# Last down-projection part of a decoder block: activations split in place, modulation rows one at a time, late x and partial-sum tiles fetched late

## Chip, cores and metric

One core of one Trainium2 chip runs the whole block. The metric is the device time of one execution in microseconds (us). The kernel before took 2182.07 us in the median of three runs.

## The reference

A decoder block in float32 with 512 tokens and 2048 channels. The part that matters here is its end:

```python
c_act = jax.nn.silu(c)
mod = c_act @ w_ada[l] + b_ada[l]
sh1, sc1, gt1, sh2, sc2, gt2 = jnp.split(mod[:, None, :], N_MOD, axis=-1)
...
h = _rmsnorm(x, norm2_g[l]) * (1.0 + sc2) + sh2
x = x + gt2 * _conv_ffn(h, w_up[l], conv_w[l], conv_b[l], w_down[l])
return _rmsnorm(x, norm_f_g)
```

`_conv_ffn` multiplies by `w_up`, convolves over three tokens, gates, and multiplies the 5632 gated channels by `w_down`. This last product, the gate vector `gt2` (the last 2048 columns of `w_ada`) and the final normalisation are the kernel's last stage.

## The kernel before

Channels lie on the 128 partitions and tokens on the free axis. Every float32 product is made of three TensorE passes (`mm3`, L133 to L135): a matrix is split into a rounded high part and the remainder, and high by high, high by low and low by high are added up in PSUM. Splitting a weight tile (`wsplit`) takes one ScalarE cast (L1373) and one VectorE subtraction (L1374); three split buffers `uw` take turns, so the split of one tile can run while two earlier ones are in use.

The 44 channel blocks of the down-projection come in three groups. Blocks 0 to 7 are a plain product, whose sums go to DRAM (`yd`). Blocks 8 to 23 are done by a Strassen-Winograd scheme (`strassen`, eight steps of seven half-width products), whose results are added to `yd` in DRAM by accumulating DMAs. Blocks 24 to 43, the last part, are 20 blocks kept as ten pairs `A3`. `act_pair` loads a pair from DRAM (`ad`) into two scratch slots of 128x512, and casts and subtracts into an operand unit that the Strassen scheme has given free; `REST` lists which unit each pair takes: first those of Y11, then Y21, T1, T2 and T3. The first four pairs are made inside the last Strassen step (`in_last`), the others in `down_four`. There are ten slots in all, which serve every short-lived 128x512 tile.

There are 16 output tiles f. For f = 0 to 3, `down_four` goes over blocks 0-7, then 8-15, then 16-19, and for each of these over the four tiles, so that the late pairs are needed late. Tiles 4 to 7 follow one by one, 512 tokens wide. Tiles 8 to 15 are done in two halves of 256 tokens (`down_half`), so that the first half can be normalised while the second is multiplied. A product over 8 blocks and 512 tokens is 24 matmuls of 128x512.

A tile's result is x + gt2 * (yd + last part). `load_x2` fetches the x tile and the `yd` tile by GpSimd's DMA queue and adds gt2*yd on VectorE (L1807); `last_residual` adds the product (L1250), takes squares on ScalarE and adds them up (L1242). The gate column comes from `gate_row`: one row block of `ada3` (128x2048, 1 MB, tile `wa2`) is loaded by SyncE's queue (L1771), multiplied by the broadcast `cact` (tile `cb2`) and summed on VectorE (L1772). Rows i and i+8 are done together in `gate_rows`, row i in buffer `y2` and row i+8 in buffer `y3` (for i under 8), each loaded just ahead of its use in the program. `gate_rows` is called five times in `down_four` and three times in tiles 4 to 6, so 16 rows are done by tile 6.

A scheduler orders each engine's instructions from the program's dependences and its own estimates. After that each engine and each DMA queue works strictly in its own order. SyncE's queue carries the weight tiles (`wd`, L1757), the activation loads (L1488) and the `ada3` rows in one line, so an issue that waits for a buffer holds up everything behind it. The weight tiles of the last part use five buffers in turn: three of tag `wide`, and the two halves of `wd2`, which lies where Y22's second operand unit was. `cb2` takes Y22's first unit, and `y2` and `y3` are T4's units.

Of the kernel before, what the change touches and what calls it, by code (L numbers as in the profile page):

```python
# [26 lines left out]
NWF = 8  # L27
# [40 lines left out]
def block_kernel(ctx, tc, a, out, stop=None, dbg=None):  # L68
    nc = tc.nc
    V, S, G, PE = nc.vector, nc.scalar, nc.gpsimd, nc.tensor  # L70
# [29 lines left out]
    def cols(name, lo, hi):  # L100
        return vec[:, COLS[name] + lo : COLS[name] + hi]
# [11 lines left out]
    mod = cp.tile([P, 96], F32, tag="mod", name="mod")  # L113
# [17 lines left out]
    def mm3(ps, wh, wl, xh, xl, start, stop, more=False):  # L131

        PE.matmul(ps, wh, xh, start=start, stop=False, skip_group_check=more)  # L133
        PE.matmul(ps, wh, xl, start=False, stop=False, skip_group_check=more)  # L134
        return PE.matmul(ps, wl, xh, start=False, stop=stop, skip_group_check=more)  # L135
# [49 lines left out]
    cact = tc.dram_tile([1, D], F32, name="cact")  # L185
# [47 lines left out]
    wa, raws, land, dma = {}, {}, {}, [3.6]  # L233
# [202 lines left out]
    cb = p0.tile([P, D], F32, tag="cb", name="cb")  # L436
# [752 lines left out]
    rb = ctx.enter_context(tc.tile_pool(name="rb", bufs=1, reuse_waits="tile"))  # L1189
# [5 lines left out]
    def bank():  # L1195
        return psm.tile([P, T], F32, tag="b", name="b")
# [14 lines left out]
    def quad(i, name, dt=F32):  # L1211
        return rb.tile([P, 4, T], dt, tag=f"x2_{i}", name=name)
# [18 lines left out]
    ea = ctx.enter_context(tc.tile_pool(name="ea", bufs=1, reuse_waits="tile"))  # L1231
# [36 lines left out]
    for k0 in range(4, KT, 4):  # L1268
# [98 lines left out]
    def wsplit(src, off=0):  # L1367
        n = src.shape[-1]
        i = nsplit[0] % 3
        nsplit[0] += 1  # L1370
        w = (ea, ea, ub)[i].tile([P, WS], F32R, tag=f"w{i}", name="uw")
        hi, lo = w[:, off : off + n], w[:, 2 * QW + off : 2 * QW + off + n]
        S.copy(hi, src)  # L1373
        lo_of[0] = V.tensor_tensor(lo, src, hi.bitcast(F32), op=ALU.subtract)  # L1374
        return hi, lo
# [83 lines left out]
    ad = [tc.dram_tile([P, T], F32, name=f"ad{j}") for j in range(NF)]  # L1459
# [14 lines left out]
    UNITS = [[(ub, f"{t}{g}") for g in range(2)] for t in ("t1", "t2", "y22", "t3")]  # L1474
    UNITS += [[(ea, "t40"), (ea, "t41")]] + [[(rb, f"y{2 * i + g}") for g in range(2)] for i in range(2)]
    FIRST = [(u, g) for u in (5, 6) for g in range(2)]
    REST = [(u, g) for u in (0, 1, 2, 3, 5) for g in range(2)]
    OPS = dict(zip(("Y11", "Y21", "T1", "T2", "Y22", "T3", "T4"), UNITS))
    ND = 8
    NR = NF - 3 * ND  # L1480

    def act_pair(i, u, g):

        pool, tag = UNITS[u][g]
        t = pool.tile([P, 2, 2, T], F32R, tag=tag, name="act2")
        for n in range(2):
            s_ = Slot("al")
            nc.sync.dma_start(s_.t, ad[2 * i + n])  # L1488
            S.copy(t[:, 0, n, :], s_.t)
# [74 lines left out]
    A1, A3 = [], []  # L1564
# [24 lines left out]
    for n, j in enumerate(order):  # L1589
        wa, wb = wq[2 * (n % 2)], wq[2 * (n % 2) + 1]  # L1590
# [137 lines left out]
            pend = (f + NWF, u2, pa, w22)  # L1728
        return pend

    def rest_pair():
        i = len(A3) // 2
        A3.extend(act_pair(3 * ND // 2 + i, *REST[i]))

    def in_last(f, i):
        if f == NWF - 1:
            rest_pair()

    plain(A1, 0)
    pend = strassen(in_last)  # L1740
# [4 lines left out]
    def down_row():  # L1745
        if nrow[0] % 5 > 2:
            w = wd2[:, nrow[0] % 5 - 3, :]
        else:
            w = wide("wd").rearrange("p a b -> p (a b)")
        nrow[0] += 1  # L1750
        return w

    def down(ps, f, acts, blocks=(0, 8, 16)):
        for k0 in blocks:
            n = min(8, NR - k0)
            w = down_row()
            nc.sync.dma_start(w[:, 0 : n * P], a["wdn"][f, :, (3 * ND + k0) * P : (3 * ND + k0 + n) * P])  # L1757
            wh, wl = wsplit(w[:, 0 : n * P], 16 if acts[0].shape[-1] == HT else 0)
            for k in range(n):
                sl = slice(k * P, (k + 1) * P)  # L1760
                x = acts[k0 + k]
                mm3(ps, wh[:, sl], wl[:, sl], x[:, 0, :], x[:, 1, :], start=k0 + k == 0, stop=k0 + k == NR - 1)

    cb = []

    def gate_row(i):
        if not cb:
            cb.append(ea.tile([P, D], F32, tag="t40", name="cb2"))
            nc.sync.dma_start(cb[0], cact[0:1, :].partition_broadcast(P))
        wa = rb.tile([P, D], F32, tag=f"y{2 + i // 8}", name="wa2")  # L1770
        nc.sync.dma_start(wa, a["ada3"][i, :, :])  # L1771
        V.scalar_tensor_tensor(wa, wa, 1.0, cb[0], op0=ALU.mult, op1=ALU.mult, accum_out=mod[:, 80 + i : 81 + i])  # L1772

    def gate_rows(f):
        with tc.issue_after(lo_of[0].ins):
            gate_row(f)
            gate_row(f + NWF)
        m = mod[:, 80:96].rearrange("p (a b) -> p a b", a=2)[:, :, f]
        V.tensor_add(m, m, cols("b_ada", 80, 96).rearrange("p (a b) -> p a b", a=2)[:, :, f])

    def down_four():

        pss = [bank() for _ in range(4)]
        for k0 in (0, 8, 16):
            while len(A3) < min(k0 + 8, NR):
                rest_pair()
# [16 lines left out]
    def load_x2(f):  # L1803
        G.dma_start(x2(f), x2d[f])
        s_ = Slot("yd")
        G.dma_start(s_.t, yd[f])
        V.scalar_tensor_tensor(x2(f), s_.t, gate(f), x2(f), op0=ALU.mult, op1=ALU.add)  # L1807
        s_.done()
# [17 lines left out]
    for f in range(NWF):  # L1826
        if f == 0:
            pss = down_four()
        elif f >= 4:
            if gated[0] < NWF:  # L1830
                gate_rows(gated[0])
                gated[0] += 1
# [6 lines left out]
    for f in range(NWF, KT):  # L1839
        down_half(0, f)  # L1840
    for f in range(NWF, KT):
        n = f - NWF
# [107 lines left out]
```

## Time and profile before

| quantity | value |
|---|---|
| median of three runs | 2182.07 us (2179.99 to 2186.82) |
| profiled execution | 2190.21 us |
| its span, first to last instruction | 2188.4 us |
| busy TensorE, VectorE, ScalarE, GpSimd | 2125.2, 1676.9, 1046.7, 232.5 us |
| HBM read, written | 432.81 MB, 36.18 MB |

The profile is of one execution and lists busy time by engine. PE is TensorE's matmuls, DVE VectorE, ACT ScalarE, POOL GpSimd, SP SyncE, and a q behind an engine means its sequencer or DMA queue. Matmuls overlap each other, so a PE that is busy all the time can still be at half its rate; counting matmuls in a stretch tells more. "a <- b" behind an idle time says that a's wait ended with b. The time outside the span (launch and end) is 1.8 us.

### The profile page before, as it was taken

To read this page: it belongs to the slowest core of one execution; us is meant where nothing else is said; L and a number is where in the kernel's file an instruction comes from. 1 tells how busy PE (TensorE), PEld (TensorE's weight loads), DVE (VectorE), ACT (ScalarE), POOL (GpSimd) and SP (SyncE) were. 2 spreads that over 40 slices of the span, in tenths; PEclk is the share of its full clock that TensorE was granted. 3 is DMA by queue.
4 is the path that set the end of the run, shared out by engine and by line. 5 is a ranking of instruction groups with operands and counts; after the bars stand their busy time and mean duration, and the time that the engine had idled before them with its cause. 6 is when DMAs were issued, how large, how long until landed. Compare 5 with 4: busy or idle time off the path is not lost.

```text
span 2188.4 us, 44045 instructions
## 1 busy us (share of the span) xinstructions
PE 2125.2 (97%) x17864; PEld 1876.5 (86%) x17864; DVE 1676.9 (77%) x2607; ACT 1046.7 (48%) x1510; POOL 232.5 (11%) x368
## 2 busy tenths in 40 slices
PE   8999999999999999999999999999999999996997
PEld 3577777777768888999999999999999899975897
DVE  7988898888853678888888887777778467768454
ACT  4354444444333466655555555555557344432353
POOL 0012111111100101110010000000000000210000
PEclk9999999999999999999999999999999999998998
DMA  9966666666437666988888877777777444698354
GB/s 392 411 215 197 193 194 178 198 184 191 118 111 260 194 200 210 276 242 247 259 245 250 227 208 204 208 207 211 208 194 229 170 143 124 197 348 314 120 180 168
DMA packets 169998, 471.90 MB, mean 216 GB/s; under 512 B 21361, under 2 KB 29505, under 8 KB 159681
## 3 DMA queue, kind: packets, MB, share of 16 engines
q1 hardware_dynamic: 121522, 354.22, 47.7%
q0 software_dynamic: 27056, 77.10, 17.0%
q10 hardware_dynamic: 21216, 37.76, 5.6%
q8 instruction: 140, 2.29, 0.4%
q14 instruction: 64, 0.52, 0.1%
HBM read 432.81 MB, written 36.18 MB: 214 GB/s over the span
## 4 chain that ended last, share of the span: by engine, by line
PE 74%; issue 10%; DMA 8%; DVE 5%; ACT 2%; POOL 1%; SPq 0%; POOLq 0%; DVEq 0%; ACTq 0%
PE b L135 15%; PE b L133 15%; PE b L134 15%; PE mm L631 10%; PE pf L412 4%; DMA wa<-ada 2%; PE b L1203 2%; PE b L1204 1%; DMA wrow<-wup 1%; DMA wraw<-win 1%; PE pb L1033 1%; DVE war L750 1%; DMA x<-dx 1%; DMA wraw<-wout 1%; DMA wd<-wdn 1%
## 5 line engine op out<-in xcount | busy, mean ns | idle before, releaser
L135 PE MATMUL b<-t,uw 128*128 128x256 f32 x1408 | 388.6, 276 | 0.0
L133 PE MATMUL b<-t,uw 128*128 128x256 f32 x1408 | 388.6, 276 | 0.0
L134 PE MATMUL b<-t,uw 128*128 128x256 f32 x1408 | 388.6, 276 | 0.0
L133 PE MATMUL b<-y,uw 128*128 128x256 f32 x1056 | 293.7, 278 | 2.7 <-ACT uw L1373 2.7
L135 PE MATMUL b<-y,uw 128*128 128x256 f32 x1056 | 293.1, 278 | 0.8 <-DVE uw L1374 0.7
L134 PE MATMUL b<-y,uw 128*128 128x256 f32 x1056 | 292.9, 277 | 0.0
L631 PE MATMUL mm<-ahl,whi 128*128 128x512 f32 x864 | 290.5, 410 | 2.0 <-DVE rk L534 1.4
L134 PEld LDWEIGHTS b<-t,uw 128*128 128x128 f32 x1408 | 264.4, 188 | 0.0
L133 PEld LDWEIGHTS b<-t,uw 128*128 128x128 f32 x1408 | 264.3, 188 | 0.0
L135 PEld LDWEIGHTS b<-t,uw 128*128 128x128 f32 x1408 | 264.3, 188 | 0.0
L1374 DVE TENSOR_TENSOR uw<-r,uw 128x1024 fp32r<-128x1024 f32 x164 | 200.3, 1222 | 77.6 <-ACT uw L1373 77.6
L1374 DVE TENSOR_TENSOR uw<-wquart,uw 128x1024 fp32r<-128x1024 f32 x156 | 190.6, 1222 | 68.1 <-ACT uw L1373 67.7
L135 PE MATMUL b<-act,uw 128*128 128x256 f32 (+1 forms) x608 | 203.8, 335 | 13.5 <-DVE uw L1374 13.5
L1374 DVE TENSOR_TENSOR uw<-wd,uw 128x1024 fp32r<-128x1024 f32 (+1 forms) x112 | 123.9, 1107 | 116.9 <-ACT uw L1373 116.9
L133 PE MATMUL b<-act,uw 128*128 128x256 f32 (+1 forms) x608 | 203.9, 335 | 6.2 <-ACT uw L1373 6.2
L1373 ACT CAST uw<-wquart 128x1024 fp32r<-128x1024 f32 x156 | 164.0, 1051 | 89.0 <-PE b L135 66.1
L134 PE MATMUL b<-act,uw 128*128 128x256 f32 (+1 forms) x608 | 203.2, 334 | 0.0
L133 PEld LDWEIGHTS b<-y,uw 128*128 128x128 f32 x1056 | 199.9, 189 | 3.3 <-ACT uw L1373 3.3
L1373 ACT CAST uw<-r 128x1024 fp32r<-128x1024 f32 x164 | 172.4, 1051 | 61.7 <-PE b L135 61.7
L135 PEld LDWEIGHTS b<-y,uw 128*128 128x128 f32 x1056 | 199.7, 189 | 1.2 <-DVE uw L1374 1.2
L134 PEld LDWEIGHTS b<-y,uw 128*128 128x128 f32 x1056 | 199.7, 189 | 0.1
L631 PEld LDWEIGHTS mm<-ahl,whi 128*128 128x128 f32 x864 | 158.6, 189 | 43.3 <-issue 12.2
(353 smaller groups left out, 4599.4 us busy)
## 6 DMA issues: line engine op xcount, KB each, us to landing
wquart<-wup SPq DMA_DIRECT2D x176, 512.0 KB, 5.3
wa<-ada SPq DMA_DIRECT2D x48, 1024.0 KB, 9.4
war<-ada SPq DMA_DIRECT2D x192, 256.0 KB, 3.7
wd<-wdn SPq DMA_DIRECT2D x64, 512.0 KB, 4.4
wraw<-win ACTq DMA_DIRECT2D x118, 256.0 KB, 4.3
wraw<-wout SPq DMA_DIRECT2D x96, 256.0 KB, 3.5
wquart<-wup POOLq DMA_DIRECT2D x44, 512.0 KB, 7.1
r<-wup SPq DMA_DIRECT2D x44, 512.0 KB, 4.6
```

The costliest lines, as they stand in the source:

```text
L133: PE.matmul(ps, wh, xh, start=start, stop=False, skip_group_check=more)
L134: PE.matmul(ps, wh, xl, start=False, stop=False, skip_group_check=more)
L135: return PE.matmul(ps, wl, xh, start=False, stop=stop, skip_group_check=more)
L412: PE.matmul(pf[n % 2 * 4 + ii], w[:, sl], full[k], start=k == 0, stop=k == KT - 1)
L631: PE.matmul(ps, w[:, sl], x, start=first, stop=k == KT - 1 and i == 2)
L750: V.scalar_tensor_tensor(wa, wa, 1.0, cqs[kq], op0=ALU.mult, op1=ALU.mult, accum_out=modq[:, kq, j : j + 1])
L1033: PE.matmul(pt[HS[e], h, c * 2 * L : (c + 1) * 2 * L], nt[HS[e], s, :], rw[HS[e], s, :, :], start=True, stop=True)
L1203: PE.matmul(ps[:, :].rearrange("p (a b) -> p a b", a=2), wh, x, start=start, stop=False)
L1204: PE.matmul(ps[:, 0:HT], wl, x[:, 0, :], start=False, stop=stop)
L1373: S.copy(hi, src)
L1374: lo_of[0] = V.tensor_tensor(lo, src, hi.bitcast(F32), op=ALU.subtract)
```

## The change

It has four parts, all in the last stage.

- The ten activation pairs are loaded into their final place. `act_pair_inplace` sends the raw block into the half of the operand tile that will hold the remainder, casts from there into the other half, and subtracts in place. No slot is used; instead the load itself now has to wait until TensorE has read the old operand. Pairs 0 to 3 are loaded by GpSimd's queue, the other six by SyncE's.
- The gate rows come one at a time, in the order 0 to 15, alternating between `y2` and `y3`. `gate_load` issues a row's load two rows ahead of its use: rows 0 and 1 after the first tile's first product, row i+2 behind row i. Five rows (instead of ten) are done in `down_four`, two with each of the tiles 4 to 7, and the rest in tiles 8 to 12 of the first half. The bias add is now one column per row (16 of 128x1 instead of 8 of 128x2).
- The broadcast `cact` load and rows 0 and 1 have a fixed place in the program.
- `load_x2(f + 8)` moves out of tiles 0 to 7 to the head of `down_half(0, f)`.

```diff
+    def act_pair_inplace(i, u, g, eng):
+        pool, tag = UNITS[u][g]
+        t = pool.tile([P, 2, 2, T], F32R, tag=tag, name="act2")
+        for n in range(2):
+            raw = t[:, 1, n, :].bitcast(F32)
+            eng.dma_start(raw, ad[2 * i + n])
+            S.copy(t[:, 0, n, :], raw)
+            V.tensor_tensor(t[:, 1, n, :], raw, t[:, 0, n, :].bitcast(F32), op=ALU.subtract)
+        return [t[:, :, n, :] for n in range(2)]
...
-    def gate_row(i):
-        if not cb:
-            cb.append(ea.tile([P, D], F32, tag="t40", name="cb2"))
-            nc.sync.dma_start(cb[0], cact[0:1, :].partition_broadcast(P))
-        wa = rb.tile([P, D], F32, tag=f"y{2 + i // 8}", name="wa2")
-        nc.sync.dma_start(wa, a["ada3"][i, :, :])
-        V.scalar_tensor_tensor(wa, wa, 1.0, cb[0], op0=ALU.mult, op1=ALU.mult, accum_out=mod[:, 80 + i : 81 + i])
...
+    def gate_load(i):
+        if i < KT:
+            wa2[i] = rb.tile([P, D], F32, tag=f"y{2 + i % 2}", name="wa2")
+            nc.sync.dma_start(wa2[i], a["ada3"][i, :, :])
+
+    def gate_row():
+        i = gated[0]
+        gated[0] += 1
         with tc.issue_after(lo_of[0].ins):
-            gate_row(f)
-            gate_row(f + NWF)
...
+            m = mod[:, 80 + i : 81 + i]
+            V.scalar_tensor_tensor(wa2[i], wa2[i], 1.0, cb[0], op0=ALU.mult, op1=ALU.mult, accum_out=m)
+            V.tensor_add(m, m, cols("b_ada", 80 + i, 81 + i))
+        gate_load(i + 2)
...
-                if (k0 == 0 and f >= 2) or (k0 == 8 and f % 2 == 0) or (k0 == 16 and f == 0):
-                    gate_rows(gated[0])
-                    gated[0] += 1
+                    cb.append(ea.tile([P, D], F32, tag="t40", name="cb2"))
+                    nc.sync.dma_start(cb[0], cact[0:1, :].partition_broadcast(P))
+                    gate_load(0)
+                    gate_load(1)
+                if k0 // 2 + f > 1 and f % 2:
+                    gate_row()
...
-        load_x2(f + NWF)
         ps = pss[f] if f < 4 else bank()
         if f >= 4:
             down(ps, f, A3)
+            gate_row()
         last_residual(f, [ps], 0, T)
     for f in range(NWF, KT):
+        if gated[0] < KT and f % 2 == 0:
+            gate_row()
+        load_x2(f)
         down_half(0, f)
```

TensorE's order stays as it was. On SyncE's queue, the rows below begin just behind the first four `ada3` rows of before, and end with the first weight tile of tile 4 (the one 128x1024 `wd`). The 128x512 `wd` rows are blocks 16-19 of tiles 0 to 3, and `al` is the last of the activation loads. Before:

```order
L1771 DMA wa_21803<-ada 128x2048
L1771 DMA wa_21806<-ada 128x2048
L1488 DMA al<-ad_9820 128x512
L1757 DMA wd_21569<-wdn 128x512
L1771 DMA wa_21868<-ada 128x2048
L1771 DMA wa_21871<-ada 128x2048
L1757 DMA wd_21569<-wdn 128x512
L1757 DMA wd<-wdn 128x512
L1771 DMA wa_21938<-ada 128x2048
L1771 DMA wa_21941<-ada 128x2048
L1757 DMA wd<-wdn 128x512
L1757 DMA wd<-wdn 128x1024
```

Now, behind the first three rows, up to the seventh; `act` is the last pair's loads:

```order
L1500 DMA act_21883<-ad_9819 128x512
L1782 DMA wa_21812<-ada 128x2048
L1500 DMA act_21883<-ad_9820 128x512
L1768 DMA wd_21561<-wdn 128x512 x2
L1768 DMA wd<-wdn 128x512 x2
L1768 DMA wd<-wdn 128x1024
L1782 DMA wa_21874<-ada 128x2048
L1768 DMA wd_21561<-wdn 128x1024
L1768 DMA wd_21561<-wdn 128x512
L1782 DMA wa_21924<-ada 128x2048
```

Tile 4's first weight tile stood behind ten `ada3` rows and stands behind four now.

On VectorE, the rows below lead up to the remainder of that same weight tile (the last `uw<-wd` row 128x1024). Before:

```order
L1374 TENSOR_TENSOR uw<-wd,uw 128x512
L1779 TENSOR_TENSOR mod<-mod,vec 128x2
L1250 SCALAR_TENSOR_TENSOR x_21570<-b,mod,x_21570 128x512 x2
L1807 SCALAR_TENSOR_TENSOR x_21571<-yd,mod,x_21571 128x512
L1807 SCALAR_TENSOR_TENSOR x_21573<-yd,mod,x_21573 128x512
L1242 TENSOR_TENSOR acc<-acc,sqx 128x512
L1250 SCALAR_TENSOR_TENSOR x_21570<-b,mod,x_21570 128x512
L1772 SCALAR_TENSOR_TENSOR wa_22045,mod<-wa_22045,cb_21695 128x2048
```

and then, behind one more L1250, one more row product L1772 (`wa_22048`), two L1242 and a bias add, `L1374 TENSOR_TENSOR uw<-wd,uw 128x1024`. Now:

```order
L1374 TENSOR_TENSOR uw<-wd,uw 128x512
L1789 SCALAR_TENSOR_TENSOR wa_21874,mod<-wa_21874,cb_21629 128x2048
L1250 SCALAR_TENSOR_TENSOR x_21562<-b,mod,x_21562 128x512
L1790 TENSOR_TENSOR mod<-mod,vec 128x1
L1789 SCALAR_TENSOR_TENSOR wa_21924,mod<-wa_21924,cb_21629 128x2048
L1242 TENSOR_TENSOR acc<-acc,sqx 128x512
L1250 SCALAR_TENSOR_TENSOR x_21562<-b,mod,x_21562 128x512
L1790 TENSOR_TENSOR mod<-mod,vec 128x1
L1822 SCALAR_TENSOR_TENSOR x_21563<-yd,mod,x_21563 128x512
L1250 SCALAR_TENSOR_TENSOR x_21562<-b,mod,x_21562 128x512
L1242 TENSOR_TENSOR acc<-acc,sqx 128x512
L1374 TENSOR_TENSOR uw<-wd,uw 128x1024
```

Two row products still stand between the last 128x512 remainder and this one, now rows 4 and 5 instead of rows 5 and 13 (the eleventh and twelfth that are done); the L1250 of tiles 1 to 3 stand there in both.

More of the change, by code (lines that the diff above doesn't have):

```diff
@@ L1729, in strassen, with rest_pair @@
         return pend
-    def rest_pair():
+    def rest_pair(eng):
         i = len(A3) // 2
-        A3.extend(act_pair(3 * ND // 2 + i, *REST[i]))
+        A3.extend(act_pair_inplace(3 * ND // 2 + i, *REST[i], eng))
     def in_last(f, i):
         if f == NWF - 1:
-            rest_pair()
+            rest_pair(G)
     plain(A1, 0)
@@ L1764, in block_kernel @@
     cb = []
-    def gate_row(i):
-        if not cb:
-            cb.append(ea.tile([P, D], F32, tag="t40", name="cb2"))
-            nc.sync.dma_start(cb[0], cact[0:1, :].partition_broadcast(P))
-        wa = rb.tile([P, D], F32, tag=f"y{2 + i // 8}", name="wa2")
-        nc.sync.dma_start(wa, a["ada3"][i, :, :])
-        V.scalar_tensor_tensor(wa, wa, 1.0, cb[0], op0=ALU.mult, op1=ALU.mult, accum_out=mod[:, 80 + i : 81 + i])
-    def gate_rows(f):
+    wa2 = {}
+    def gate_load(i):
[5 more added lines that the diff above has]
+        gated[0] += 1
         with tc.issue_after(lo_of[0].ins):
-            gate_row(f)
-            gate_row(f + NWF)
-        m = mod[:, 80:96].rearrange("p (a b) -> p a b", a=2)[:, :, f]
-        V.tensor_add(m, m, cols("b_ada", 80, 96).rearrange("p (a b) -> p a b", a=2)[:, :, f])
+            m = mod[:, 80 + i : 81 + i]
+            V.scalar_tensor_tensor(wa2[i], wa2[i], 1.0, cb[0], op0=ALU.mult, op1=ALU.mult, accum_out=m)
+            V.tensor_add(m, m, cols("b_ada", 80 + i, 81 + i))
+        gate_load(i + 2)
     def down_four():
@@ L1785, in down_four @@
             while len(A3) < min(k0 + 8, NR):
-                rest_pair()
+                rest_pair(nc.sync)
             for f in range(4):
```

6 lines of the change are left out of this document (2 added, 4 removed).

## Prediction

> **What bounds the kernel now.** I read the windows of the last 290 us first, then the waits, then the chain of waits. Each window row gives its length, then the busy time and count of PE, PEld, DVE, ACT and POOL, the granted TensorE clock, the DMA share and GB/s.
>
> ```profile
> 1922.24:1960.64 38.40, 36.71 (x172) 29.90 (x171) 22.33 (x26) 9.52 (x13) 6.75 (x11) 1.00 0.96 350
> 1960.64:1978.70 18.06, 13.46 (x58) 10.81 (x58) 15.41 (x18) 2.40 (x5) 2.18 (x4) 0.95 0.95 346
> 1978.70:2007.40 28.70, 16.29 (x49) 12.09 (x50) 24.07 (x31) 8.87 (x13) 2.74 (x5) 0.68 0.90 336
> 2007.40:2059.17 51.77, 51.77 (x229) 42.86 (x228) 26.14 (x31) 14.67 (x17) 0.00 (x0) 1.00 0.44 143
> 2059.17:2171.60 112.43, 112.43 (x967) 112.28 (x965) 63.73 (x85) 59.64 (x80) 0.00 (x0) 1.00 0.56 183
> 1922.24 0.40 PE L133 MATMUL b<-act,uw 128*128 128x512 f32 x1
> 2059.17 0.28 PE L133 MATMUL b<-act,uw 128*128 128x256 f32 x1
> L135 PE MATMUL b<-act,uw 128*128 128x512 f32 x160 | 64.5, 403 | 12.5 <-DVE uw L1374 12.5
> 1902.40:1922.24 19.84, 17.08 (x146) 16.87 (x145) 14.76 (x21) 13.91 (x22) 4.18 (x7) 1.00 0.96 309
> ```
>
> The 512-token part runs from 1922.24 to 2059.17, so 136.9 us. Its fourth window is full: 229 matmuls in 51.77 us, 0.226 us each. In the part, three passes of 160 matmuls take 480 x 0.226 = 108.5 us. The Strassen scheme's last product, 24 matmuls of 128x256, also lies in it: the last row gives (19.84 - 2.76) / 146 = 0.117 us each, where 2.76 us is a wait quoted below, so 2.8 us. Pure work is 111.3 us; 25.6 us are lost. They fall in the second and third windows, where 58 and 49 matmuls stand in 46.8 us, while the DMA engines are over 90% busy at about 340 GB/s. Before and after, TensorE sets the pace.
>
> Who is waited for (total, times, longest):
>
> ```profile
> PE b L135 <- DVE uw L1374: 12.5, 4, 11.2
> PE b L133 <- ACT uw L1373: 6.2, 3, 4.6
> PE b L133 <- ACT cap L1705: 2.8, 1, 2.8
> SPq L1771 <- DVE wa L1772: 50.9, 13, 6.9
> ...
> 1968.68 7.34 DMA wa<-ada
> ...
> 1976.05 1.95 DVE wa L1772
> ...
> 1978.38 7.33 DMA wa<-ada
> ...
> 1985.73 1.29 DVE wa L1772
> ...
> 1988.95 11.33 DMA wd<-wdn
> 1999.36 1.05 ACT L1373 CAST uw<-wd 128x1024 fp32r<-128x1024 f32 x1 [5.24 <-DMA wd<-wdn]
> 2001.65 2.95 DVE L1374 TENSOR_TENSOR uw<-wd,uw 128x1024 fp32r<-128x1024 f32 x3
> ```
>
> PE waits for split weights, these for weight loads, and these for SyncE's queue, which spends 50.9 us waiting until DVE has used up an `ada3` row and freed its buffer. The chain shows this ring: load 7.3, product 2.3, the next load, a round of 1978.38 - 1968.68 = 9.7 us for two rows. Weight loads get through only between rounds; tile 4's (issued 1988.95) lands 11.3 us later.
>
> **The change part by part.** Prices, from the groups and the DMA issues (KB, median us to landing):
>
> ```profile
> L1772 DVE SCALAR_TENSOR_TENSOR wa<-wa,cb 128x2048 f32<-128x2048 f32 x16 | 36.6, 2288 | 11.1 <-DMA wa<-ada 11.0
> L1374 DVE TENSOR_TENSOR uw<-wd,uw 128x1024 fp32r<-128x1024 f32 x18 | 21.9, 1221 | 23.5 <-ACT uw L1373 23.5
> L1807 DVE SCALAR_TENSOR_TENSOR x<-yd,mod,x 128x512 f32<-128x512 f32 x16 | 11.6, 746 | 0.1
> L1250 DVE SCALAR_TENSOR_TENSOR x<-b,mod,x 128x512 f32<-128x512 f32 x8 | 5.9, 746 | 1.6 <-PE b L135 1.6
> L1242 DVE TENSOR_TENSOR acc<-acc,sqx 128x512 f32<-128x512 f32 x6 | 4.1, 687 | 2.9 <-ACT sqx L1241 2.7
> wa<-ada SPq DMA_DIRECT2D x15, 1024.0 KB, 7.4
> wd<-wdn SPq DMA_DIRECT2D x8, 512.0 KB, 9.7
> yd<-yd POOLq DMA_DIRECT2D x14, 256.0 KB, 6.8
> ```
>
> *Rows spread out.* Tile 4's first weight load now stands behind four rows instead of ten: three rounds, 29 us, leave its way, more than the whole loss, so something else comes last. Walking the new order: the last Strassen product ends 8 us after the part's start, near 1930, and frees both buffers. Row 0 lands near 1938 and is used by 1941; only then does SyncE issue row 2 and, behind it, the weights of tiles 2 and 3 for blocks 8-15. With 9.7 us they land at 1951 and are split by 1954. Without waits PE reaches tile 2 there at 1922.2 + 2.8 + 6 x 5.43 = 1957.6. That fits with 3 us to spare. The last activation pair waits for row 1 (used near 1948) and lands at 1956; its remainder precedes tile 3's on DVE, done by 1959 against a need at 1963. Blocks 16-19 end at 1979.5.
>
> There one wait stays. DVE's order has row products 4 and 5, then the last L1250, which needs tile 3's product, and an L1242 ahead of tile 4's remainder. From 1979.5: L1250 0.75, L1242 0.69, L1374 1.22, so 2.7 us; under 0.5 of it is hidden by the two passes that need no remainder. I take 2.7. Tiles 4 to 7 need 13.6 us each (60 x 0.226) and use two rows each, a ring of 9.7, with remainders ordered well ahead: nothing more. Expected loss in the part: 2.7 instead of 25.6, a gain of 22.9.
>
> The clock: the third window was granted 0.68 because of an 11.2 us wait, while the 2.76 us wait near 1916 left the clock at 1.00. A stall of 2.7 should leave it too. The Trainium skill's page "TensorE: Matmul & The Clock Gate", What's actually happening, puts the drop to half rate behind one idle window of about 3.4 us. By that rule, too, 2.7 us costs no clock; a stall a little longer would add some 2.3 us.
>
> *x and `yd` of late tiles.* Eight `yd` loads (2 MB) and, by 1979.5, four rows fewer (4 MB) leave the saturated stretch: about 6 MB, 18 us at 340 GB/s. The `x` loads stay early in GpSimd's queue. What must land from 1918 to 1979.5 is about 18 MB (six rows 6.3, weights 4.7, eleven `act` loads 2.9, `cb2` 1, four `x` tiles 1, five `yd` loads 1.3, two stores 0.5, by the KB of the rows; blocks 0-7 of tiles 0 and 1 are there already): 53 us of 61. That is the thin cover; each load that lands late by more than 3 us costs its excess. I allow 2 us, between 0 and 8 (if the mean rate were 275 GB/s, 18 MB would take 65 us, 4 us too many, and the clock another 4).
>
> *Half stage.* It takes two row products and eight L1807 more, 10.6 us of DVE, beside 63.73 busy of 112.43.
>
> ```profile
> 2070.35 1.23 DVE L1374 TENSOR_TENSOR uw<-wd,uw 128x1024 fp32r<-128x1024 f32 x1 [1.68 <-ACT uw L1373]
> 2073.18 1.23 DVE L1374 TENSOR_TENSOR uw<-wd,uw 128x1024 fp32r<-128x1024 f32 x1 [1.60 <-ACT uw L1373]
> ```
>
> A tile of 7 us leaves DVE two holes, 1.68 and 1.60. A row product, placed ahead of a remainder, pushes it by 2.3 - 1.7 = 0.6, and PE comes to it 1.8 us later: 0, at most 2.
>
> *Activations in place.* Pairs 0 to 3 can now be requested only when Y11's and Y21's last products are read, and GpSimd issues them in order behind x tiles and a store of `yd`.
>
> ```profile
> 1899.59 2.18 POOL L1804 DMA_DIRECT2D x<-x2d x4 [0.98 <-DVE uw L1374]
> 1915.73 0.62 ACT L1489 CAST act<-al 128x512 fp32r<-128x512 f32 x1 [4.60 <-DMA al<-ad]
> 1916.67 0.39 PE L133 MATMUL b<-Y,uw 128*128 128x256 f32 x1 [2.76 <-ACT cap L1705]
> x<-x2d POOLq DMA_DIRECT2D x4, 256.0 KB, 7.3
> ```
>
> Before, a cast waits 4.6 us for a slot's load and PE loses 2.76. Now: Y11 is read by 1902.4, pair 0 lands near 1907, its casts hold up ACT's copy to 1908.5, the store behind it, and pairs 2 and 3 until 1909.3; these land near 1915, and T2's split and the copy behind their casts cost PE about 2 us. So the 2.8 turns into 2: I count 0, between -3 (landing 3 us later) and +2.8. The ACT wait of the other loads (0.7 to 1.6 us at 1936) is in the 25.6 already.
>
> **Sum.** 22.9 - 2 = 21 against the profiled execution's 2190.2 us, so 2169. That execution is 8.1 us over the median; part of the excess may be just this stall, so I take 19 off the median: 2163.
>
> **The rivals.** (a) The transfers still bind: landings slip past their 3 us cover in blocks 8-19, with another clock drop. Loss 10 to 15, gain 8 to 14: 2168 to 2174. The 0.95 DMA share speaks for it, the 6 MB taken out against it. Chance 0.17. (b) Nothing comes of it: rows that wait in DVE's order hold up the remainders, in tiles 4 to 7 instead of 0 to 3 (eight rows there instead of six). It needs rounds over 13.6 us where 9.7 were seen. Gain 0 to 6: 2176 to 2182. Chance 0.11. (c) Slower: GpSimd's queue. It is in order, and the first eight activation loads and twelve x loads stand in it with the stores between. The rows show 2.18 / 4 = 0.55 us per issue; were it four times that while DVE works (14.76 of 19.84 us in the step), twelve issues would take 26 us, pair 3 would land at 1942, and the part would begin 20 us late, with a clock drop: 25 lost against 21 won, 2186 or more. It decides from the point where pair 3 lands after about 1940. The Trainium skill's page "DMA: Bandwidth & Descriptors", SWDGE vs HWDGE vs iDMA, speaks for this rival: GpSimd writes its descriptors into SBUF and is locked out while DVE is in its two-port mode, and SyncE's loads are immune. The steady 0.55 us with DVE busy shows no lock here. Chance 0.07. (d) The Strassen wait goes as well, and tile 4's is hidden: gain 28, 2154. Chance 0.06.
>
> **How the numbers follow.** Forecast 0.59 (2157 to 2168), and the rivals as above. The range 2154 to 2174 holds the forecast, (a) and (d): 0.82. A difference under 0.3%, 6.5 us, is about what cannot be told from none. Faster 0.82, same 0.11, slower 0.07.
>
> **What would show it.** Right: SyncE's wait for row products far under 50.9 us and no longer followed by PE; about 57 us from the part's start to the last of tiles 0 to 3; one PE wait of 2 to 3 us before tile 4; clock 1.00 throughout; the half stage at 112 us. Wrong: PE waits over 4 us in blocks 8-19 (then a), or waits for VectorE in tiles 4 to 7 (b), or the first matmul on `act` later than 1925 (c).

## The result and the profile after

The kernel after takes 2167.7 us (median of 20 executions, 2163.7 to 2203.5), the kernel before 2186.5 in the same comparison (20 executions); the ratio is 0.9911, 95% interval 0.9882 to 0.9939. Some executions of every kernel but the last one tried are about 30 us longer than the others, so the medians in the table of experiments are those of the executions within 0.8% of a kernel's shortest (2184.0 before and 2166.6 after, 17.4 apart), and the profiles of "ten single rows" and "half rows and stores", which are of such longer executions, are read only from the last Strassen step on, behind the extra time. The profiled execution of after took 2164.5 us with a span of 2162.7.

Its windows, with the columns of those of before (length, then busy time and count of PE, PEld, DVE, ACT, POOL, the granted clock, DMA share and GB/s): the last Strassen step, the four tiles of `down_four` in two pieces, the stall at tile 4, the rest of the 512-token part, and the half stage.

```profile
1897.23:1917.54 20.31, 17.43 (x147) 17.03 (x146) 13.32 (x16) 11.24 (x18) 7.47 (x14) 1.00 0.97 320
1917.54:1955.94 38.40, 38.40 (x183) 32.28 (x182) 23.70 (x30) 15.13 (x21) 5.61 (x9) 1.00 0.99 367
1955.94:1975.00 19.06, 19.06 (x85) 15.79 (x85) 16.19 (x23) 7.13 (x10) 1.09 (x2) 1.00 0.91 315
1975.00:1982.43 7.43, 5.06 (x15) 3.70 (x15) 7.43 (x10) 2.84 (x5) 0.55 (x1) 0.77 0.81 288
1982.43:2033.50 51.07, 51.07 (x227) 42.23 (x225) 37.26 (x48) 14.66 (x17) 3.28 (x6) 1.00 0.83 288
2033.50:2145.76 112.26, 112.26 (x966) 112.21 (x965) 69.64 (x93) 59.63 (x80) 0.00 (x0) 1.00 0.56 184
```

The 512-token part is 2033.50 - 1917.54 = 115.96 us, 20.97 shorter than before's 136.93. TensorE is busy in all of it but one place of 7.43 us. Where before had 107 matmuls in 46.8 us, the corresponding stretch is full. Of the part's 115.96 us, 4.7 are above the 111.3 of pure work. The half stage is as long as before.

Who TensorE and SyncE's queue wait for (total, times, longest). PE's waits are those from 1880 us on without the two at the very end, SyncE's those from 1915 to 2010; L1374 and the uw lines are where they were, before's L1705 is now L1716, L1757 (weight load) L1768, L1771 (row load) L1782 and L1772 (row product) L1789:

```profile
PE b L135 <- DVE uw L1374: 3.1, 2, 2.4
PE b L133 <- ACT cap L1716: 2.2, 1, 2.2
```

```profile
SPq L1768 <- DVE uw L1374: 34.3, 15, 5.0
SPq L1782 <- DVE mod L1790: 22.0, 5, 10.6
SPq L1782 <- DVE wa L1789: 10.5, 5, 2.5
```

In place of 12.5 us for remainders and 6.2 for casts, PE waits 3.1 for remainders. SyncE still waits 32.5 us for row products, in two entries (one ends with the bias add L1790 right behind the product); but what it mostly waits for now is the weight buffer it is about to fill, so weights come as early as their buffers allow.

The one stall of the part, on PE and then on VectorE:

```profile
1975.04 0.39 PE L134 MATMUL b<-act,uw 128*128 128x512 f32 x1
1977.80 0.50 PE L135 MATMUL b<-act,uw 128*128 128x512 f32 x1 [2.37 <-DVE uw L1374]
...
1979.51 0.63 PE L135 MATMUL b<-act,uw 128*128 128x512 f32 x1
1979.94 0.63 PE L133 MATMUL b<-act,uw 128*128 128x512 f32 x1
...
1982.47 0.40 PE L133 MATMUL b<-act,uw 128*128 128x512 f32 x1
```

```profile
1971.06 2.28 DVE L1789 SCALAR_TENSOR_TENSOR wa<-wa,cb 128x2048 f32<-128x2048 f32 x1
...
1974.60 0.74 DVE L1822 SCALAR_TENSOR_TENSOR x<-yd,mod,x 128x512 f32<-128x512 f32 x1
1975.27 0.74 DVE L1250 SCALAR_TENSOR_TENSOR x<-b,mod,x 128x512 f32<-128x512 f32 x1
1975.93 0.68 DVE L1242 TENSOR_TENSOR acc<-acc,sqx 128x512 f32<-128x512 f32 x1
1976.53 1.22 DVE L1374 TENSOR_TENSOR uw<-wd,uw 128x1024 fp32r<-128x1024 f32 x1
```

Tile 3's residual (L1250), a norm step (L1242), then tile 4's remainder: PE loses 2.76 - 0.23 = 2.5 us. Behind it matmuls start 0.43 us apart instead of 0.23 until 1982.4: the clock is at half.

The spans differ by 25.7 us, which is 21.0 in the part, 5.2 ahead of the last Strassen step (it begins at 1902.40 before, at 1897.23 after) and -0.5 in that step. The change touches nothing ahead of the step, nor does any variant below; yet in their profiles (the two of longer executions apart) the step begins anywhere from 1896 to 1906. So the 5.2 us are not the change's, and the medians, 17 to 19 apart, bear that out.

### The profile page after: what moved, and what is told of

It is laid out like the page before. It is cut to its first block, busy times and chain, and to the rows that moved or that the text cites. A ratio compares the mean times of both kernels' runs of the same rounds, so it can differ in the third digit from the quotient of the medians.

```text
span 2162.7 us, 44015 instructions
## 1 busy us (share of the span) xinstructions
PE 2118.8 (98%) x17864; PEld 1874.0 (87%) x17864; DVE 1677.9 (78%) x2615; ACT 1046.7 (48%) x1510; POOL 236.2 (11%) x376
## 4 chain that ended last, share of the span: by engine, by line
PE 87%; DMA 4%; DVE 4%; ACT 2%; issue 2%; POOL 0%; DVEq 0%; SPq 0%; ACTq 0%; POOLq 0%
PE b L135 19%; PE b L133 19%; PE b L134 19%; PE mm L631 11%; PE pf L412 4%; PE b L1203 2%; PE b L1204 1%; DMA wrow<-wup 1%; PE pb L1033 1%; DVE war L750 1%; DMA wraw<-wout 1%; DMA wa<-ada 1%; PE pa L697 0%; ACT x L1303 0%; PE pf L133 0%
## 5 line engine op out<-in xcount | busy, mean ns | idle before, releaser
L1374 DVE TENSOR_TENSOR uw<-r,uw 128x1024 fp32r<-128x1024 f32 x164 | 200.4, 1223 | 79.1 <-ACT uw L1373 79.1
L1374 DVE TENSOR_TENSOR uw<-wquart,uw 128x1024 fp32r<-128x1024 f32 x156 | 190.7, 1223 | 68.0 <-ACT uw L1373 67.7
L1374 DVE TENSOR_TENSOR uw<-wd,uw 128x1024 fp32r<-128x1024 f32 (+1 forms) x112 | 123.9, 1108 | 105.6 <-ACT uw L1373 105.3
```

## The experiments

Theory: too much stood ahead of tile 4's weights and remainders in two in-order queues, SyncE's (row loads) and VectorE's (row products), so the number and place of the rows made the gain. First rival: the bytes taken out of a saturated stretch. Second rival: the in-place loads, or GpSimd's queue that issues them. "Part" is the 512-token part in the profiled execution, "to tile 4" its start to the first matmul of tile 4 (57.3 without a wait), "against before" the median minus that of the kernel before, measured beside it (2183.1 to 2184.0). The ratio with its interval is formed over more executions than the two medians, so it can differ from their quotient by up to 0.3%; differences of a few us between variants are within these intervals, and rest on the trace.

| kernel | part | to tile 4 | median | against before | ratio, 95% |
|---|---|---|---|---|---|
| before | 136.93 | 68.87 | 2184.0 | | |
| after | 115.96 | 57.28 | 2166.6 | -17.4 | 0.9911 (0.9882 to 0.9939) |
| slots kept | 115.98 | 57.28 | 2168.1 | -15.1 | 0.9929 (0.9894 to 0.9964) |
| in place only | 132.15 | 73.45 | 2182.4 | -0.7 | 0.9995 (0.9949 to 1.0041) |
| late x only | 126.39 | 68.91 | 2177.7 | -5.4 | 0.9980 (0.9935 to 1.0025) |
| rows on GpSimd | 134.85 | 69.84 | 2192.9 | +9.7 | 1.0048 (1.0003 to 1.0093) |
| ten single rows | 123.06 | 62.92 | 2175.8 | -7.7 | 0.9940 (0.9891 to 0.9989) |
| more bytes | 124.67 | 65.70 | 2176.3 | -7.3 | 0.9988 (0.9934 to 1.0042) |
| pairs by SyncE | 115.87 | 57.28 | 2170.1 | -13.5 | 0.9931 (0.9887 to 0.9975) |
| residuals later | 111.71 | 57.31 | 2163.8 | -19.8 | 0.9915 (0.9870 to 0.9961) |
| half rows | 130.25 | 66.86 | 2183.0 | -1.0 | 0.9978 (0.9951 to 1.0006) |
| half rows and stores | 137.67 | 74.75 | 2189.4 | +5.4 | 1.0027 (0.9985 to 1.0069) |
| casts later | 111.68 | 57.28 | 2167.6 | -16.3 | 0.9895 (0.9851 to 0.9939) |

The first matmul of tile 4 is not yet the one that waits in every kernel: in before and after the wait stands behind it, since only the third pass needs the remainder.

**Slots kept.** The kernel after, its activation pairs again through slots and SyncE.

```diff
-        A3.extend(act_pair_inplace(3 * ND // 2 + i, *REST[i], eng))
+        A3.extend(act_pair(3 * ND // 2 + i, *REST[i]))
```

> The changed kernel with the activation pairs loaded through slots by SyncE's queue, as before; rows and late tiles as changed. Theory (too many ada3 rows stood ahead of the weights and remainders of tiles 0 to 4, in SyncE's and VectorE's order): 16 to 20 us faster than before, the 512-token part of the last stage under 119 us. Rival (the slots: loads that waited for a free slot cost the time): under 8 us faster, the part over 128 us.

The part is the same to 0.02 us and the median 1.5 us longer (15.1 faster than before, just under the 16 expected). The in-place pairs are not where the gain comes from.

**In place only.** The kernel before with that part of the change alone.

```diff
-                rest_pair()
+                rest_pair(nc.sync)
...
-            rest_pair()
+            rest_pair(G)
```

> The kernel before with the activation pairs loaded in place and nothing else changed. Theory (rows ahead of the weights): within 4 us of before, the 512-token part 133 to 138 us. Rival (slots): 10 us faster or more, the part under 127 us.

No difference (-0.7 us), from the other side the same answer. Its part is 4.8 us shorter than before's profiled one at an equal median, so one profile of a kernel with stalls like these says its part only to some 5 us.

**Late x only.** The kernel before, the `x` and `yd` tiles of f = 8 to 15 fetched in the half stage.

```diff
-        load_x2(f + NWF)
...
     for f in range(NWF, KT):
+        load_x2(f)
         down_half(0, f)
```

> The kernel before with only the x and yd tiles of tiles 8 to 15 moved to the half stage; rows in pairs as before. Theory (rows ahead of the weights): 0 to 4 us faster, SyncE's queue still waits some 50 us for row products. Rival (bytes: the DMA engines are full, so what leaves the stretch is won): 2 MB of yd at 340 GB/s, so 6 us, and up to 6 us of VectorE's eight adds with it, 6 to 12 us faster.

-5.4 us lies between the two expectations: more than I gave it, though the interval of the ratio doesn't exclude none. It takes 2 MB of `yd` from the stretch and eight L1807 (8 x 0.75 = 6.0 us) from VectorE's order as well, so by itself it doesn't say which of the two counts.

**Rows on GpSimd.** The kernel before, the row loads issued by GpSimd, so that no weight load stands behind a row in SyncE's queue.

```diff
-        nc.sync.dma_start(wa, a["ada3"][i, :, :])
+        G.dma_start(wa, a["ada3"][i, :, :])
```

> The kernel before with the ada3 rows loaded by GpSimd's queue instead of SyncE's; same bytes, same order on VectorE. Theory in its queue half (weights stood behind rows on SyncE's queue): SyncE no longer waits for row products; the part loses 8 to 15 us instead of 25.6, since VectorE's order still has twelve row products ahead of tile 4's remainder; 8 to 15 us faster. Theory in its VectorE half alone (the rows' ring ahead of the remainders binds): 0 to 4 us. Rival (bytes): 0, the DMA engines are as full as before.

Slower by 9.7 us, where all three expectations had 0 to 15 us faster. In the profiles the part is 2.1 us shorter than before's and the last Strassen step 3.9 longer; before's profiled execution lies 6.2 us over its median, this one 1.4 under, so the profiles show less of the difference. SyncE waits for rows no more: what is left is mostly the weights' own wait for buffers. PE still loses 12.5 us to remainders, 8.7 of it at tile 4. SyncE's waits, PE's waits, ScalarE's cast of tile 4's first weights, and VectorE up to their remainder:

```profile
SPq L1757 <- DVE uw L1374: 48.3, 10, 11.4
```

```profile
PE b L135 <- DVE uw L1374: 12.5, 4, 8.7
```

```profile
1993.63 1.03 ACT L1373 CAST uw<-wd 128x1024 fp32r<-128x1024 f32 x1
```

```profile
1994.30 2.28 DVE L1772 SCALAR_TENSOR_TENSOR wa<-wa,cb 128x2048 f32<-128x2048 f32 x1
...
1998.68 2.29 DVE L1772 SCALAR_TENSOR_TENSOR wa<-wa,cb 128x2048 f32<-128x2048 f32 x1 [0.83 <-DMA wa<-ada]
...
2002.90 1.22 DVE L1374 TENSOR_TENSOR uw<-wd,uw 128x1024 fp32r<-128x1024 f32 x1
```

The cast is done at 1994.7, and the remainder starts at 2002.9: the weights are there and VectorE is late, with two row products, one of them waiting for its load, and the residuals and norm steps between them to do first. So SyncE's queue alone is not the cause; the half of the theory that holds at tile 4 is VectorE's order. The test isn't a clean one: the rows now stand in GpSimd's queue, and VectorE waits 11.9 us for them here.

**Ten single rows.** The kernel after with ten row products ahead of tile 4's remainder (after has six, before twelve, ten of them with loads ahead of tile 4's first weights), but one at a time and with loads two ahead, as in after.

```diff
-                if k0 // 2 + f > 1 and f % 2:
+                if k0 // 2 + f > 1 and k0 // 2 + f < 12:
                     gate_row()
```

> The kernel after, with ten row products ahead of tile 4 instead of six, each still placed singly with the two-deep loads of the kernel after (ten of sixteen rows there, as in the kernel before). The theory (the number of rows that stand ahead of tile 4's weights and remainder sets the loss): five rounds of 9.7 us from about 8 us after the part's start end near 57 us, and tile 4's first weights are issued only then and need some 10 us to land, so PE waits 8 to 14 us around tile 4 and the clock falls once or twice more (1.7 to 3.4 us each): the 512-token part 126 to 132 us, time 2177 to 2185. Rival (single rows between other work and loads asked for two ahead are what helped, not their number): part under 119, time within 3 us of the kernel after's 2167.

9.2 us slower than after, with a part of 123.06, 3 us less than my theory's lower end and 4 more than the rival's upper. The ring of load and product, from which I took 126 to 132, doesn't set the pace: VectorE waits 3.6 us for rows in all. PE has two waits in the part. The first, of 3.3 us at 1999.6, is one of SyncE's queue: the last pair's loads and the weights of blocks 16-19 are issued from 1991.4 on, right behind a row load that had waited for VectorE to free its buffer, and ScalarE idles 5.6 us until the first of them lands. The second, of 3.8 us at tile 4, is again one of order; ScalarE's cast of these weights was done at 2008.9:

```profile
2008.51 2.29 DVE L1789 SCALAR_TENSOR_TENSOR wa<-wa,cb 128x2048 f32<-128x2048 f32 x1 [0.53 <-DMA wa<-ada]
...
2011.45 2.28 DVE L1789 SCALAR_TENSOR_TENSOR wa<-wa,cb 128x2048 f32<-128x2048 f32 x1
...
2015.66 1.21 DVE L1374 TENSOR_TENSOR uw<-wd,uw 128x1024 fp32r<-128x1024 f32 x1
```

The number of rows matters, then, in both queues. But four more rows are 4.2 MB more too, so the next kernels take rows and bytes apart.

**More bytes.** The kernel after with 6.3 MB of stores that nobody reads.

```diff
                 rest_pair(nc.sync)
+                for n in (-2, -1):
+                    dump = tc.dram_tile([P, 2, T], F32, name=f"dump{len(A3) + n}")
+                    G.dma_start(dump, A3[n].bitcast(F32))
```

> The kernel after, with twelve more stores of 512 KB (6.3 MB, each a finished half of an activation pair, to memory that nobody reads) on GpSimd's queue while tiles 0 to 3 run: about the bytes that the change was said to take out of that stretch. The theory (queue and VectorE order decide, transfers have room): at most one late landing, 0 to 4 us slower than the kernel after, 2167 to 2171, part 116 to 120. Rival (transfers bind: fewer bytes were the gain): 6.3 MB at 340 GB/s are 18.5 us, of which at most the slack of a few us is hidden: 10 us slower or more, 2177 or more, part over 126, the PE waits for split weights in blocks 8 to 19.

The part grows by 8.7 us and the median by 9.7: far outside my expectation, and close under the rival's (10 us or more, a part over 126). The transfers between the part's start and tile 4 (the share by slices and rows of loads: KB each, median us to landing), first of after, then of this kernel:

```profile
DMA packets 5659, 20.05 MB, mean 350 GB/s; under 512 B 695, under 2 KB 695, under 8 KB 4644
...
wd<-wdn SPq DMA_DIRECT2D x8, 512.0 KB, 6.9
act<-ad SPq DMA_DIRECT2D x8, 256.0 KB, 9.5
```

```profile
DMA packets 7275, 25.76 MB, mean 392 GB/s; under 512 B 869, under 2 KB 869, under 8 KB 6309
...
dump<-act POOLq DMA_DIRECT2D x11, 512.0 KB, 11.1
wd<-wdn SPq DMA_DIRECT2D x8, 512.0 KB, 11.2
act<-ad SPq DMA_DIRECT2D x6, 256.0 KB, 14.7
```

The engines, over 90% busy in both, move 12% more per us when more is asked of them, and the loads of weights and of activation pairs take 4 to 5 us longer (those of rows, at 7.8 us, only 0.2). After is close under the edge: its transfers are hidden, but not by far.

**Half rows,** the kernel before with half of each row's bytes and the same order and work on VectorE, and **half rows and stores,** the same with the bytes put back as stores.

```diff
-        nc.sync.dma_start(wa, a["ada3"][i, :, :])
-        V.scalar_tensor_tensor(wa, wa, 1.0, cb[0], op0=ALU.mult, op1=ALU.mult, accum_out=mod[:, 80 + i : 81 + i])
+        nc.sync.dma_start(wa[:, 0 : D // 2], a["ada3"][i, :, 0 : D // 2])
+        for _ in range(2):
+            V.scalar_tensor_tensor(wa[:, 0 : D // 2], wa[:, 0 : D // 2], 1.0, cb[0][:, 0 : D // 2], op0=ALU.mult, op1=ALU.mult, accum_out=mod[:, 80 + i : 81 + i])
```

```diff
+                for n in (-2, -1) if len(A3) < NR else ():
+                    dump = tc.dram_tile([P, 2, T], F32, name=f"dump{len(A3) + n}")
+                    G.dma_start(dump, A3[n].bitcast(F32))
```

> The kernel before, with only the first half of each ada3 row loaded (512 KB in place of 1 MB) and the product taken twice over that half, so that VectorE's time stays; it leaves out the second half of the 16 gate sums. Order and number of the rows on SyncE and VectorE are those of before, ten ahead of tile 4. Theory of the ring (rows in the way in order): only the load's part of the round shrinks, by some 2 of 9.7 us, five rounds, so the part falls from 136.9 to 125 to 130 and PE still waits before tile 4. Theory of the bytes (5.2 MB fewer in the stretch, 15 us at 340 GB/s): the part falls to 119 or less, the time to 2170 or less.

> The half rows of the kernel above, and ten stores of 512 KB (finished activation pairs, to memory that nobody reads) on GpSimd's queue in the same stretch, so that the bytes are again those of before while rows land from half the size; it leaves out the second half of the gate sums as well. Ring: as with half rows alone, within 4 us in the part and the time. Bytes: the gain of the half rows goes again, part 132 or more and the time within 4 us of before's 2184.

Taking 5.2 MB out of the kernel before, with the order left, gives 1.0 us in the median and 6.7 in the part: by bytes it should have been 119 or less, and it is 130.25, just over the 125 to 130 of the ring. As before's profiled execution lies 6.2 us over its median and this one at it, the median is the better measure of the two: by it nearly all of the loss stays. The transfers have room there (row of the windows from the part's start to tile 4), and VectorE again reaches tile 4's remainder behind row products:

```profile
1922.24:1989.10 66.86, 61.38 (x266) 49.74 (x265) 49.18 (x79) 16.35 (x22) 8.58 (x15) 0.95 0.85 282
```

```profile
1988.34 1.22 DVE L1773 SCALAR_TENSOR_TENSOR wa<-wa,cb 128x1024 f32<-128x1024 f32 x1
...
1991.90 1.21 DVE L1773 SCALAR_TENSOR_TENSOR wa<-wa,cb 128x1024 f32<-128x1024 f32 x1
...
1994.37 1.22 DVE L1374 TENSOR_TENSOR uw<-wd,uw 128x1024 fp32r<-128x1024 f32 x1
```

With the stores, the part is 7.4 us longer again and the median 6.4: adding bytes costs nearly as much as it did in after, and the prediction of the ring (no difference) missed. So the two are not alternatives. Order is enough for a loss of 19 us (130.25 - 111.3) with the DMA share at 0.85; bytes are enough to add 9 with few rows. The change lowers both. That it has to lower the order is shown; for the bytes it is shown only that 6.3 MB more would cost, which is more than the 3.6 MB that the change takes out up to tile 4 (23.6 MB before, 20.05 after).

**Pairs by SyncE.** The kernel after, the first four pairs requested by SyncE.

```diff
-            rest_pair(G)
+            rest_pair(nc.sync)
```

> The kernel after, with the first four activation pairs loaded in place by SyncE's queue instead of GpSimd's. The theory (the issuing queue of these eight loads does not matter to the sum): within 2 us of the kernel after, 2165 to 2169, the copy of T2's product in the last Strassen step still 1.5 to 3 us late. Rival (GpSimd's queue, with x loads and a store ahead, holds the casts and through them PE): the 2.2 us wait for the copy goes and the clock with it, 3 us or more faster. The other side: SyncE waits for Y11 and Y21 to be read ahead of the first weights of the 512-token part, which then come late: 3 us or more slower, the wait for split weights at the part's start.

3.5 us slower, none of the three quite: the copy's wait goes, but a remainder of T2's product comes late behind the pairs' subtractions, PE waits 2.20 us for it in the step and then has 6.8 us of half clock. The two intervals overlap, so slower isn't certain; nothing shows that asking by GpSimd costs time here.

**Residuals later.** The kernel after, tile 3's residual and norm, with those of tiles 0 to 2, behind tile 4's product.

```diff
-        last_residual(f, [ps], 0, T)
+        if f >= 4:
+            for r in range(4 if f == 4 else 0):
+                last_residual(r, [pss[r]], 0, T)
+            last_residual(f, [ps], 0, T)
```

> The kernel after, with the residual and norm steps of tiles 0 to 3 put behind tile 4's product instead of ahead of it, so that VectorE comes to tile 4's remainder without waiting for tile 3's last product. The theory (the 2.4 us wait at tile 4 is VectorE's order alone, and it costs the clock 1.7 us behind it): both go, part about 112, 4 us faster, 2163. Rival (the weights of tile 4 land late, or row 5's product ahead of it still waits for its load): the wait stays within 1 us of 2.4 and the time within 1.5 us of 2167.

The stall and the half clock behind it are gone. The windows before and behind tile 4's first matmul, and VectorE there:

```profile
1921.19:1978.51 57.32, 57.32 (x267) 47.90 (x266) 39.25 (x51) 20.56 (x28) 5.63 (x9) 1.00 0.93 336
1978.51:2032.91 54.40, 54.40 (x242) 45.06 (x241) 45.76 (x59) 19.20 (x24) 4.38 (x8) 1.00 0.90 321
```

```profile
1974.93 2.29 DVE L1789 SCALAR_TENSOR_TENSOR wa<-wa,cb 128x2048 f32<-128x2048 f32 x1 [0.82 <-DMA wa<-ada]
...
1977.22 1.22 DVE L1374 TENSOR_TENSOR uw<-wd,uw 128x1024 fp32r<-128x1024 f32 x1
```

The part is 111.71 us, 0.4 above pure work: 4.25 less than after, and 2.8 in the median. It has the lowest median of all kernels here; its lead over after rests on the trace and the two medians, since the intervals of the ratios (0.9870 to 0.9961, after 0.9882 to 0.9939) overlap.

**Casts later.** That kernel, and in the last Strassen step each pair's casts one product behind its load, so that ScalarE's copy should not stand behind a cast that waits.

```diff
         if f == NWF - 1:
+            if late:
+                late.pop()()
-            rest_pair(G)
+            rest_pair(G, True)
```

> The kernel with the residuals of tiles 0 to 3 behind tile 4's product, and of the four activation pairs that the last Strassen step loads, each cast and remainder put one product later than its load's request (the last behind the step), so that ScalarE's copy of T2's product stands ahead of casts that wait for their load. Theory (the 2 to 3 us that PE waits in that step are ScalarE's order): the waits of 2.75 and 1.05 us between the step's products fall to under 1 together, part 112, 2 to 3 us faster than with the residuals alone, 2160 to 2162. Rival (the split weights of T2 or the loads themselves are late): the step's time and the median stay within 1 us, 2162.5 to 2164.5.

The expectation missed: 2167.6 (six executions, and a ratio whose interval overlaps the last kernel's), the step 24.5 us long in place of 20.7, with one wait of 3.6 for the copy and half clock behind it. ScalarE still holds the copy behind a cast, now of the next load:

```profile
1915.51 0.62 ACT L1505 CAST act<-act 128x512 fp32r<-128x512 f32 x1 [3.91 <-DMA act<-ad]
1916.97 0.62 ACT L1505 CAST act<-act 128x512 fp32r<-128x512 f32 x1 [0.85 <-DMA act<-ad]
1917.50 0.37 ACT L1725 COPY cap<-b 128x256 f32<-128x256 f32 x1
```

One product, 2.8 us, is less than the 6 to 8 us that these loads take. How this step's 2 to 3 us could be saved stays open.

## Why the prediction came out as it did

**The size of the gain.** Forecast 2163 with a gain of 19 in the median; measured 2167.7, a gain of 17 to 19. Nearly all of the 4.7 us between the two times are before's own: its median came out at 2186.5 over 20 executions, not at 2182.07. The part was to fall by 22.9 less 2; it fell by 21.0, and the loss left in it is 4.7 us, as the sum had it, though of other pieces (below).

**Rows spread out: right in what, wrong in where.** The step that failed is "these for SyncE's queue" as the account of the wait at tile 4, and with it the ring as the pace. Before's own trace shows it. The load "issued 1988.95" is not the one that this wait needed: tile 4's first weights were cast by 1989.7, two matmuls on them ran from 1991.11 on, and it is their remainder, which the third needs, that starts only at 2001.65. ScalarE's cast, and VectorE on the way:

```profile
1988.62 1.05 ACT L1373 CAST uw<-wd 128x1024 fp32r<-128x1024 f32 x1 [0.94 <-DVE uw L1374]
```

```profile
1992.53 2.28 DVE L1772 SCALAR_TENSOR_TENSOR wa<-wa,cb 128x2048 f32<-128x2048 f32 x1
...
1996.00 2.28 DVE L1772 SCALAR_TENSOR_TENSOR wa<-wa,cb 128x2048 f32<-128x2048 f32 x1
...
2000.97 0.69 DVE L1242 TENSOR_TENSOR acc<-acc,sqx 128x512 f32<-128x512 f32 x1 [2.68 <-ACT sqx L1241]
```

From the cast's end to 1998.3 VectorE is busy with what stands ahead in its order; then it waits 2.7 us for a square on ScalarE, which stands behind the cast of the next weight tile. Only these last 2.7 us are a late landing. The experiments agree: with SyncE's queue freed of rows, PE waits 17.4 us for casts and remainders in place of 18.7; with rows of half the size, three quarters of the part's loss stay. In each, and with ten single rows, tile 4's remainder starts behind row products, residuals and norms in VectorE's order. SyncE's 50.9 us were for the most part a sign of the same thing: it waited for VectorE, and still waits 32.5 us for rows in after, where no matmul of tiles 0 to 3 waits for weights. One piece of that reading stands: in blocks 16-19 before's PE waits 4.6 and 1.0 us for casts whose weights were issued late, at 1969.1 and 1978.8, each right behind a row load that had waited for its buffer. What the prediction did carry through, the walk along VectorE's order to "L1250 0.75, L1242 0.69, L1374 1.22", is the step that gave the right wait: 2.7 forecast, 2.5 lost, at the place named, and gone when those two come later.

**The clock: wrong.** "A stall of 2.7 should leave it too" failed: 3.4 us at half clock, 1.7 us lost (2.3 were named for a stall a little longer). The evidence was one wait of 2.76 that had cost no clock. The last section shows why it was not enough.

**Transfers: allowed 2, cost 0.** No matmul of tiles 0 to 3 waits for weights. The cover was thin, as said, and "more bytes" puts a figure on it: 6.3 MB, 18 us at 350 GB/s, more, and 8.4 us of them come through to tile 4. Of the bytes the estimate was off: from the start to tile 4 before moved 343 x 68.87 = 23.6 MB and after 20.05, so 3.6 MB left, not 6, and the 20.05 stand against 18 counted, since eight rows are asked for by then, not six. That the 2 us allowed here and the clock's 1.7 nearly cancel is luck.

**x and `yd` late** were counted for their bytes only. Alone they give 5.4 us by the medians, about a third of the gain, and the medians make a ladder: late loads -5.4, with them in-place pairs and single rows -7.7, with six rows instead of ten -17.4, with the residuals later -19.8. The largest step is the number of rows, with their bytes.

**Half stage: right,** 112.26 us against 112.43, with 5.9 us more of DVE in it (10.6 were counted).

**Last Strassen step: right,** 20.31 us against 19.84, +0.5 where 0 was taken from -3 to +2.8; over the other profiles the step takes 21.1 to 21.5 us with slots (rows on GpSimd apart, 23.7) and 19.3 to 22.9 with pairs in place and cast at once. The wait for the slot's load became, as the step had it, two others: 0.70 for T2's remainder and 2.18 for ScalarE's copy, which stands behind these casts:

```profile
1909.29 0.62 ACT L1501 CAST act<-act 128x512 fp32r<-128x512 f32 x1 [3.77 <-DMA act<-ad]
1910.84 0.62 ACT L1501 CAST act<-act 128x512 fp32r<-128x512 f32 x1 [0.93 <-DMA act<-ad]
1911.36 0.36 ACT L1716 COPY cap<-b 128x256 f32<-128x256 f32 x1
```

**The rivals.** (a) didn't happen, but 6.3 MB more bring it about. (b) didn't happen in tiles 4 to 7; as an account of before it was nearer than my forecast's. (c) didn't happen: the part begins without a wait on a pair, and SyncE in GpSimd's place is no faster. The Trainium skill's page "DMA: Bandwidth & Descriptors", SWDGE vs HWDGE vs iDMA, let one fear a lockout of GpSimd by VectorE; no run here shows one, with four of GpSimd's activation loads issued in 2.49 us while DVE was busy 13.32 of the step's 20.31 us; as the trace doesn't tell in which port mode VectorE's instructions ran, this is no test of it. (d) asked for both stalls to be hidden; "residuals later" hides one of them.

## What to carry to other kernels

In a chain of waits, check that the load it names fills the tile that the waiting instruction reads. Where a tensor engine waits for split weights, look at what stands ahead of the split on the in-order engine that makes it, and count instructions that could come later, before blaming the queue that loads them: a queue that waits for that engine's buffers shows the same loss a second time. Undo order and bytes separately: the same stall can need both to be low, and a load that is hidden tells nothing of how near the edge it is until bytes are added. A short wait that cost no clock once is no promise that an equal one will not.

## What the runs showed of the hardware that was not expected

The clock is judged in fixed windows. In the 13 traces (before, after and eleven variants), every stretch at half clock but the one that the end cuts off lasts a whole multiple of 3.413 us, and within an execution all of them begin on one grid of that step. For this count I laid each execution's grid over the time from 1860 to 2110 us and took the windows in which the profile shows TensorE idle for over 0.5 us: all 28 with over 2.15 us of idleness are followed by a window at half clock; of 18 between 1.6 and 2.15, 12 are; of 38 with less, 3 are, each inside a stretch that was at half already. So where a wait falls decides. Before's 2.76 us wait, in the windows of its grid, and after's 2.37 us wait with the window behind it:

```profile
1912.00:1915.41 3.41, 1.91 (x17) 1.70 (x15) 0.00 (x0) 0.00 (x0) 0.00 (x0) 1.00 0.91 326
1915.41:1918.82 3.41, 2.15 (x18) 2.15 (x19) 2.44 (x4) 3.09 (x7) 0.00 (x0) 1.00 1.02 390
```

```profile
1975.61:1979.02 3.41, 1.22 (x5) 1.05 (x6) 3.41 (x5) 2.23 (x4) 0.55 (x1) 1.00 0.92 357
1979.02:1982.43 3.41, 3.41 (x9) 2.65 (x8) 3.41 (x5) 0.00 (x0) 0.00 (x0) 0.50 0.76 232
```

The first is cut in two, 1.5 and 1.3 us of idleness, and neither half is enough; the second leaves 2.2 us in one window, and the next is at 0.50. The Trainium skill's page "TensorE: Matmul & The Clock Gate", What's actually happening, tells of a free-running activity window of about 3.4 us, and the grid agrees with it; its rule that one idle window drops the clock does not, since here 2.2 us of 3.41 do. As the grid's place against the waits differs from trace to trace, the same wait of 2 to 4 us should cost half a window, 1.7 us, in some executions and nothing in others, and a part of the spread between executions could be that; with one trace of each kernel, neither is shown.
